# Order of small TensorE products in a two-layer hybrid decoder trunk on one core

## Chip, cores, metric

One NeuronCore of a Trainium2 chip runs the whole program. The metric is device time in microseconds (us) of one execution. All inputs and outputs are float32.

## What is computed

Two layers over 256 tokens and a width of 1024. The first half of each layer is a mixer with four parallel branches, the second half a gated feed-forward block:

```
for each of 2 layers:
  z  = rmsnorm(h) @ w_in            # columns: RWKV-7 | attention | mLSTM | HGRN2 | 4 gates
  y_b = mixer_b(z_b)                # four causal mixers, heads of width 64
  h += (sum_b sigmoid(gate_b) * (y_b @ P_b)) @ w_out
  h += conv_ffn(rmsnorm(h))
```

The RWKV-7 mixer is a recurrence over a 64x64 state per head, done here in four chunks of 64 tokens:

```
sa = S a_t ;  S = S * w_t + sa b_t + v_t k_t ;  y_t = S r_t
```

## The kernel before

**Main stream.** All large products go through `mm3` (lines 343 to 345). Each factor is split into a high and a low part, and three products are added: high times high, high times low, low times high. A weight group is loaded by SyncE's DMA queue, split by ScalarE (`hi`, L298) and VectorE (`lo`, L299) into one of four buffers each, up to three groups ahead of its use. These products (gate, at, ml, up, dn and so on) use the whole 128x128 array.

**Side work.** The mixers are Python generators: `rwkv`, `hgrn`, `attn`, `ml_gate` with `mlstm`. `step()` is called inside the main stream and advances them by a pace for each, up to the next `yield`. A list scheduler then sets the final order on each engine, and each engine runs its own list strictly from front to back. So a small product stands at a fixed place between main products, and TensorE waits there if its inputs are late.

**Shapes of the small products.** Two heads share a 128-partition tile: one has partitions 0 to 63, the other 64 to 127. A product whose contraction has 64 rows uses one half of the array's rows; one with 64 output partitions uses one half of its columns. A float32 product appears as two matmul records in the trace, a transpose and a main product as one.

**The places the change touches.** In `rwkv`: `pl` (L763), four blocks per layer, pair n of heads and head par, each four products of 64 rows by 128 columns, then the masked copy `LR` (L765) by VectorE. Then the chain over chunks j = 0 to 3 (L842 to L887): `prr` = a times state S (L848, 64 rows), the sum in `LV` (L849), `pu` (L858), its two copies into `UV`, `psS` (L867, 128 rows by 64 columns), the new S (L880, VectorE), and the output `pyy`. `pyy` adds r times S (L873, 64 rows) and LR times UV (L874, 128 rows) in one accumulation for each of four heads, and ScalarE copies it to `yt` (L886). PSUM for this branch is two banks (`RWB = 2`), for the other branches three.

In `hgrn`: `pdg` (L1023) and `pdl` for h = 64 and 128 (L1050, L1053), head after head; `qsb` (L999, L1002) by VectorE is an input of `pdl`. In `attn`: the scores `psA`, `psB` (L1136), head after head, with up to 256 keys in one product. In `mlstm`: the scores `pS` (L1261, L1262). `y_out` (L569 to L574) transposes the finished mixer outputs (`pyC`, `pyA`) and splits them into `yhC`, `ylC`, which the projection `pp` of the main stream reads.

Of the kernel before, what the change touches and what calls it, by code (L numbers as in the profile page):

```python
# [9 lines left out]
F32 = mybir.dt.float32  # L10
# [3 lines left out]
OP = mybir.AluOpType  # L14
# [205 lines left out]
def trunk(tc, x, wst, prm, rows, lora, fing, cfd, cid, out, dbg=None, depth=DEPTH):  # L220
# [9 lines left out]
    PS = {}  # L230
# [248 lines left out]
    for l in range(depth):  # L479
        with ExitStack() as lx:  # L480
# [11 lines left out]
            with ExitStack() as mxs:  # L492
# [129 lines left out]
                def rwkv():  # L622
# [133 lines left out]
                    LR = rw.tile([128, 2, 2, 4, 2, 64], F32, name="LR", tag="w8")  # L756
                    lm = C("lmask")[:, None, :].to_broadcast([128, 4, 128])
                    for n in range(2):
                        for par in range(2):
                            q0 = par * 64  # L760
                            pl = PS["rw"].tile([128, 4, 128], F32, name="pl", tag="rw")
                            for j in range(4):
                                te.matmul(pl[:, j, :], bk[q0:q0 + 64, n, j].rearrange("p a b -> p (a b)"),  # L763
                                          ar[q0:q0 + 64, n, j].rearrange("p a b -> p (a b)"), start=True, stop=True)
                            ve.tensor_tensor(LR[:, n, par].rearrange("p j a t -> p j (a t)"), pl, lm, op=OP.mult)  # L765
                            yield
# [74 lines left out]
                    S, py = None, None  # L841
                    for j in range(4):  # L842
                        Rs = LV[:, :, j, :]
                        if j:
                            prr = PS["rw"].tile([128, 2, 64], F32, name="prr", tag="rw")
                            for n in range(2):
                                for q in (0, 64):
                                    te.matmul(prr[q:q + 64, n, :], ar[q:q + 64, n, j, 0, :], S[q:q + 64, n, :], start=True, stop=True)  # L848
                            ve.tensor_tensor(Rs, Rs, prr, op=OP.add)  # L849
# [12 lines left out]
                        if j < 3:  # L862
                            psS = PS["rw"].tile([128, 2, 64], F32, name="psS", tag="rw")
# [4 lines left out]
                        py = PS["rw"].tile([128, 2, 64], F32, name="pyy", tag="rw")  # L868
# [65 lines left out]
                def hgrn(zz, sp):  # L934
# [80 lines left out]

                    pds = []
                    for par in range(2):
                        pd = PS["mx"].tile([128, 4, 64], F32, name="pdg", tag="mx")
                        pds.append(pd)
                        for e in range(4):  # L1020
                            for pj in range(2):
                                sl = slice(e * 128 + pj * 64, e * 128 + pj * 64 + 64)
                                te.matmul(pd[pj * 64:pj * 64 + 64, e, :], kfl[par * 64:par * 64 + 64, sl], qfl[par * 64:par * 64 + 64, sl],  # L1023
                                          start=True, stop=True)
                    for par in range(2):
                        for pj in range(2):
# [5 lines left out]
                    while h <= 128:  # L1032
# [9 lines left out]
                                              qs[:, e * 2 + pj].rearrange("p a t -> p (a t)"), start=True, stop=True)  # L1042
                        else:
                            for par in range(2):
                                r0 = par * 64
                                pd = PS["mx"].tile([128, 4, 128], F32, name="pdl", tag="mx")
                                pds.append(pd)
                                for e in range(4):
# [74 lines left out]
                def attn(zz, sp):  # L1123
                    qk, V = zz["qk"], zz["v"]
                    am = C("amask").rearrange("p (g s) -> p g s", g=3)

                    PTs = [sp.tile([128, 3, 384], F32, name=f"PT{j}") for j in range(2)]
                    for th, j in [(th, j) for th in range(2) for j in range(2)]:
                        n_ = 128 * (th + 1)
                        r0 = j * 64  # L1130
                        S = sp.tile([128, 3, 256], F32, name="S_at", tag="S_at", bufs=2)
                        psA = PS["mx"].tile([128, 512], F32, name="psA", tag="mx")
                        psB = PS["mx"].tile([128, 512], F32, name="psB", tag="mx") if th else None
                        for g in range(3):
                            dst = psA[:, g * n_:(g + 1) * n_] if (th == 0 or g < 2) else psB[:, 0:256]
                            te.matmul(dst, qk[r0:r0 + 64, g, th * 128:(th + 1) * 128], qk[r0:r0 + 64, 3 + g, 0:n_], start=True, stop=True)  # L1136
                        Sv = S[:, :, 0:n_]
                        if th == 0:
                            ve.tensor_tensor(Sv, psA[:, 0:384].rearrange("p (g s) -> p g s", g=3), am[:, :, 128:256], op=OP.add)
                        else:  # L1140
                            ve.tensor_tensor(Sv[:, 0:2, :], psA.rearrange("p (g s) -> p g s", g=2), am[:, 0:2, :], op=OP.add)
                            ve.tensor_tensor(Sv[:, 2, :], psB[:, 0:256], am[:, 2, :], op=OP.add)
# [97 lines left out]
                def mlstm(zz, sp):  # L1240
# [17 lines left out]
                    for hd in range(4):  # L1258
                        n, r0 = hd // 2, (hd % 2) * 64
                        pS = PS["mx"].tile([128, 512], F32, name="pS", tag="mx")  # L1260
                        te.matmul(pS[:, 0:256], cv[r0:r0 + 64, 2 + n, 0:128], cv[r0:r0 + 64, n, :], start=True, stop=True)  # L1261
                        te.matmul(pS[:, 256:384], cv[r0:r0 + 64, 2 + n, 128:256], cv[r0:r0 + 64, n, 128:256], start=True, stop=True)  # L1262
                        ve.scalar_tensor_tensor(W[:, hd, :], pS[:, 0:384], 0.125 * 0.25, W[:, hd, :], op0=OP.mult, op1=OP.mult)
                        if hd % 2:
                            yield
# [238 lines left out]
```

## Time and profile before

| | |
|---|---|
| median of 3 runs | 972.03 us (969.34 to 972.32) |
| the profiled execution | 971.28 us, of it 969.5 us span |
| TensorE busy | 948.9 us, 98% |
| VectorE busy | 738.7 us, 76% |
| ScalarE busy | 564.5 us, 58% |
| GpSimd busy | 231.5 us, 24% |
| granted TensorE clock, mean | 0.989 |

A matmul's recorded duration covers its way through the array, and records overlap. So the cost of a product is the distance from its start to the next start, and that is how all rows of TensorE are read below. The span minus the time of the run is 1.8 us outside the first and last instruction.

### The profile page before, as it was taken

To read this page: it belongs to the slowest core of one execution; us is meant where nothing else is said; L and a number is where in the kernel's file an instruction comes from. 1 tells how busy PE (TensorE), PEld (TensorE's weight loads), DVE (VectorE), ACT (ScalarE), POOL (GpSimd) and SP (SyncE) were. 2 spreads that over 40 slices of the span, in tenths; PEclk is the share of its full clock that TensorE was granted. 3 is DMA by queue.
4 is the path that set the end of the run, shared out by engine and by line. 5 is a ranking of instruction groups with operands and counts; after the bars stand their busy time and mean duration, and the time that the engine had idled before them with its cause. 6 is when DMAs were issued, how large, how long until landed. Compare 5 with 4: busy or idle time off the path is not lost.

```text
span 969.5 us, 21763 instructions
## 1 busy us (share of the span) xinstructions
PE 948.9 (98%) x8860; PEld 889.9 (92%) x8860; DVE 738.7 (76%) x1180; ACT 564.5 (58%) x953; POOL 231.5 (24%) x228
## 2 busy tenths in 40 slices
PE   7999999999999999999999999999999999999996
PEld 5989998989999999999998999898999999999885
DVE  6899765568688998876698986655787889888643
ACT  6874445555466676665578534455645667766533
POOL 3500221112207721110060004100222473111101
PEclk9999999999999999999999999999999999999999
DMA  7644353433456465556555344433345647655551
GB/s 256 198 145 149 106 164 120 142 117 129 158 186 212 146 221 196 196 185 201 192 189 169 126 133 149 132 132 121 113 147 186 204 136 225 197 191 192 190 190 65
DMA packets 48979, 160.08 MB, mean 165 GB/s; under 512 B 5872, under 2 KB 7408, under 8 KB 48752
## 3 DMA queue, kind: packets, MB, share of 16 engines
q1 hardware_dynamic: 46944, 155.55, 48.8%
q10 hardware_dynamic: 1584, 2.10, 0.7%
q8 instruction: 69, 1.13, 0.5%
q0 software_dynamic: 352, 1.06, 0.4%
q14 instruction: 30, 0.25, 0.1%
HBM read 156.06 MB, written 1.05 MB: 162 GB/s over the span
## 4 chain that ended last, share of the span: by engine, by line
PE 78%; DVE 9%; POOL 6%; ACT 2%; issue 2%; DMA 2%; SPq 0%; POOLq 0%; ACTq 0%; DVEq 0%
PE up L344 7%; PE up L345 7%; PE up L343 7%; PE gate L343 5%; PE gate L345 5%; PE gate L344 5%; PE dn L345 4%; PE dn L343 4%; PE dn L344 4%; POOL sl L438 4%; DVE lo L299 2%; POOL xsc L1381 2%; PE pp L343 1%; PE pp L345 1%; PE wo L344 1%
## 5 line engine op out<-in xcount | busy, mean ns | idle before, releaser
L299 DVE TENSOR_TENSOR lo<-raw,hi 128x1024 fp32r<-128x1024 f32 (+4 forms) x314 | 373.6, 1193 | 145.9 <-ACT hi L298 144.9
L298 ACT CAST hi<-raw 128x1024 fp32r<-128x1024 f32 (+4 forms) x314 | 308.3, 984 | 283.6 <-PE gate L344 69.1
L344 PE MATMUL up<-sl,hi 128*128 128x256 f32 x576 | 160.4, 279 | 3.6 <-POOL sl L438 3.5
L345 PE MATMUL up<-sh,lo 128*128 128x256 f32 x576 | 159.9, 278 | 0.0
L343 PE MATMUL up<-sh,hi 128*128 128x256 f32 x576 | 159.7, 278 | 0.0
L343 PE MATMUL gate<-sh,hi 128*128 128x256 f32 x512 | 147.3, 288 | 0.0
L345 PE MATMUL gate<-sh,lo 128*128 128x256 f32 x512 | 144.4, 282 | 0.0
L344 PE MATMUL gate<-sl,hi 128*128 128x256 f32 x512 | 144.1, 281 | 0.0
L344 PEld LDWEIGHTS up<-sl,hi 128*128 128x128 f32 x576 | 108.9, 189 | 4.6 <-POOL sl L438 4.6
L345 PEld LDWEIGHTS up<-sh,lo 128*128 128x128 f32 x576 | 108.9, 189 | 0.1
L343 PEld LDWEIGHTS up<-sh,hi 128*128 128x128 f32 x576 | 108.8, 189 | 0.0
L343 PEld LDWEIGHTS gate<-sh,hi 128*128 128x128 f32 x512 | 97.8, 191 | 3.2 <-issue 0.7
L345 PEld LDWEIGHTS gate<-sh,lo 128*128 128x128 f32 x512 | 97.7, 191 | 1.5 <-issue 0.8
L344 PEld LDWEIGHTS gate<-sl,hi 128*128 128x128 f32 x512 | 97.7, 191 | 0.5
L1406 POOL TENSOR_TENSOR af<-sf,cvf 128x256 f32<-128x256 f32 x44 | 42.6, 970 | 161.6 <-ACT sf L1404 161.5
L1402 DVE SCALAR_TENSOR_TENSOR cvf<-up,pr,cvf 128x255 f32<-128x255 f32 (+1 forms) x144 | 69.0, 479 | 2.6
L553 POOL TENSOR_TENSOR merged<-merged,gt 128x512 f32<-128x512 f32 x16 | 24.6, 1545 | 102.1 <-DVE gt L551 82.1
L345 PE MATMUL dn<-ahi,lo 128*128 128x256 f32 x176 | 48.5, 276 | 0.0
L344 PE MATMUL dn<-alo,hi 128*128 128x256 f32 x176 | 48.5, 276 | 0.0
L343 PE MATMUL dn<-ahi,hi 128*128 128x256 f32 x176 | 48.4, 276 | 0.0
L1399 ACT ACTIVATE cvf<-up,pr 128x256 f32<-128x256 f32 x72 | 40.4, 561 | 1.6 <-DVE cvf L1402 1.6
L438 POOL TENSOR_TENSOR sl<-xsc,sh 128x256 fp32r<-128x256 f32 x32 | 39.2, 1259 | 0.0
(466 smaller groups left out, 2377.0 us busy)
## 6 DMA issues: line engine op xcount, KB each, us to landing
raw<-in_wst_dram SPq DMA_DIRECT2D x254, 512.0 KB, 3.3
raw<-in_wst_dram SPq DMA_DIRECT2D x28, 256.0 KB, 2.9
raw<-in_wst_dram SPq DMA_DIRECT2D x16, 448.0 KB, 3.2
raw<-in_wst_dram SPq DMA_DIRECT2D x8, 392.0 KB, 3.1
zrot<-zrot ACTq DMA_DIRECT2D x24, 64.0 KB, 3.1
cft<-in_cf_dram SPq DMA_DIRECT2D x1, 1041.0 KB, 6.8
hT<-in_x_dram SPq DMA_DIRECT2D x4, 256.0 KB, 5.3
raw<-in_wst_dram SPq DMA_DIRECT2D x8, 128.0 KB, 2.4
```

Source lines behind the costliest of these rows:

```text
L298: ac.copy(hi[:, c], r[:, c])
L299: ve.tensor_tensor(lo[:, c], r[:, c], hi[:, c].bitcast(F32), op=OP.subtract)
L343: te.matmul(o, lh, rh, start=first, stop=False)
L344: te.matmul(o, lh, rl, start=False, stop=False)
L345: te.matmul(o, ll, rh, start=False, stop=last)
L438: gp.tensor_tensor(lo[:, m, :], tmp, h[:, m, :].bitcast(F32), op=OP.subtract)
L553: gp.tensor_tensor(mo, mo, g, op=OP.add)
L1381: gp.tensor_tensor(xsc[:, m, :], xsc[:, m, :], R, op=OP.mult)
L1399: ac.activation(cv[:, n, :], z[:, n, :], AF.Identity, bias=P("fcb", cj), scale=P("fcw", 88 + cj))
L1402: ve.scalar_tensor_tensor(cv[:, n, d:], z[:, n, 0:T - d], P("fcw", 44 * i + cj), cv[:, n, d:], op0=OP.mult, op1=OP.add)
L1406: gp.tensor_tensor(a_, s, cv[:, 0, :], op=OP.mult)
```

## The change

In the RWKV chain, `prr` and `pyy` share one bank (`pry`), and `pu` and `psS` another. Both products with the state (a times S and r times S) are issued in one run of eight; LR times UV follows later, after `psS`, and completes the second half. Elsewhere the products with 64 rows are issued so that the two heads alternate, each head into its own bank: `pl`, `pdg`, `pdl` for h at least 64, the attention scores (also cut to 128 keys each, with one more `yield`), and the mLSTM scores. No operation of VectorE, ScalarE or GpSimd is added.

```diff
                     for n in range(2):
+                        pls = [PS["rw"].tile([128, 4, 128], F32, name="pl", tag="rw") for _ in range(2)]
+                        for j in range(4):
+                            for par in range(2):
+                                q0 = par * 64
+                                te.matmul(pls[par][:, j, :], bk[q0:q0 + 64, n, j].rearrange("p a b -> p (a b)"),
...
                         for par in range(2):
-                            q0 = par * 64
-                            pl = PS["rw"].tile([128, 4, 128], F32, name="pl", tag="rw")
-                            for j in range(4):
...
+                            ve.tensor_tensor(LR[:, n, par].rearrange("p j a t -> p j (a t)"), pls[par], lm, op=OP.mult)
+                        yield
+                        yield
...
+                        pry = PS["rw"].tile([128, 2, 2, 64], F32, name="prr", tag="rw")
+                        py = pry[:, 1]
                         if j:
-                            prr = PS["rw"].tile([128, 2, 64], F32, name="prr", tag="rw")
...
+                            for a in range(2):
+                                for n in range(2):
+                                    for q in (0, 64):
+                                        te.matmul(pry[q:q + 64, a, n, :], ar[q:q + 64, n, j, a, :], S[q:q + 64, n, :],
+                                                  start=(a == 0 or n == 0), stop=(a == 0))
+                            ve.tensor_tensor(Rs, Rs, pry[:, 0], op=OP.add)
...
-                        pu = PS["rw"].tile([128, 2, 64], F32, name="pu", tag="rw")
+                        pus = PS["rw"].tile([128, 2, 2, 64], F32, name="pu", tag="rw")
+                        pu, psS = pus[:, 0], pus[:, 1]
...
                         for n in range(2):
                             for par in range(2):
                                 q = par * 64
-                                if j:
-                                    te.matmul(py[q:q + 64, n, :], ar[q:q + 64, n, j, 1, :], S[q:q + 64, n, :], start=True, stop=False)
-                                te.matmul(py[q:q + 64, n, :], LR[:, n, par, j, 1, :], UV[:, j, n, par, :], start=(j == 0), stop=True)
+                                te.matmul(py[q:q + 64, n, :], LR[:, n, par, j, 1, :], UV[:, j, n, par, :], start=(j == 0), stop=(j == 0 or n == 1))
...
+                    for e in range(4):
+                        for pj in range(2):
+                            sl = slice(e * 128 + pj * 64, e * 128 + pj * 64 + 64)
+                            for par in range(2):
+                                te.matmul(pds[par][pj * 64:pj * 64 + 64, e, :], kfl[par * 64:par * 64 + 64, sl], qfl[par * 64:par * 64 + 64, sl],
...
+                    def scores(th, sb, Ss):
+                        pa = [PS["mx"].tile([128, 3, 128], F32, name="psA", tag="mx") for _ in range(2)]
+                        for g in range(3):
+                            for j in range(2):
+                                r = slice(j * 64, j * 64 + 64)
+                                te.matmul(pa[j][:, g, :], qk[r, g, th * 128:(th + 1) * 128], qk[r, 3 + g, sb * 128:(sb + 1) * 128],
...
+                    for n in range(2):
+                        pSs = [PS["mx"].tile([128, 512], F32, name="pS", tag="mx") for _ in range(2)]
+                        for c in range(2):
+                            for par in range(2):
+                                te.matmul(pSs[par][:, c * 256:256 + c * 128], cv[r, 2 + n, c * 128:c * 128 + 128], cv[r, n, c * 128:], start=True, stop=True)
```

Line numbers shift: `psS` is L875 in the changed kernel and bears the name of its bank, `pu`; r times S and a times S are L855, LR times UV is L879, both named `prr`.

**TensorE, RWKV chain, chunk 1 of layer 0.** The rows are instructions in program order, with the line, the operation, the tile written and the tiles read, and a count of products. `ml` and `mlt` are main products. Before:

```order
L345 MATMUL ml_2547<-sh,lo_2480 128x256
L867 MATMUL psS<-UV,bkT 64x64 x4
L873 MATMUL pyy<-S,ar 64x64
L874 MATMUL pyy<-UV,LR 64x64
L873 MATMUL pyy<-S,ar 64x64
L874 MATMUL pyy<-UV,LR 64x64
```

and two more such pairs. Now:

```order
L345 MATMUL ml_2556<-sh,lo_2485 128x256
L875 MATMUL pu<-UV,bkT 64x64 x4
L879 MATMUL prr<-UV,LR 64x64 x4
L343 MATMUL mlt_2638<-hi_2514,sh 128x512
L344 MATMUL mlt_2638<-lo_2515,sh 128x512
```

The products with S have moved ahead of `pu`, into one run of eight (`L855 ... x8`), and the eight products after `UV` stand in one run without a change of form.

**VectorE, end of the HGRN2 levels, layer 0.** `qsb_900` is the input of the last `pdl` (h = 128), `lo` a weight split, `qkat` the attention's rotated q and k. Before:

```order
L789 COPY_PREDICATED TT<-cit,LR 32x256 x2
L1002 TENSOR_TENSOR qsb_900<-zhq,thf 128x256
L792 STREAM_TRANSPOSE T__1430<-TT 128x256
L299 TENSOR_TENSOR lo_1451<-raw_1343,hi_1450 128x1024
L1112 TENSOR_TENSOR qkat<-at_1342,cft 128x512
```

Now:

```order
L998 TENSOR_TENSOR kt_839<-zhf,Q 128x2x128
L299 TENSOR_TENSOR lo_1451<-raw_1349,hi_1450 128x1024
L1118 TENSOR_TENSOR qkat<-at_1348,cft 128x512
L1007 TENSOR_TENSOR qsb_900<-zhq,thf 128x256
L299 TENSOR_TENSOR lo_1481<-raw_1379,hi_1480 128x784
```

The last `qsb` has moved behind a weight split and behind `qkat`; the copies `TT` and the transpose stand earlier.

**TensorE, end of the mLSTM and RWKV branches, layer 0.** Before:

```order
L343 MATMUL gate_3263<-sh,hi_3193 128x256
L569 MATMUL pyC<-ident_t,y_ml 128x128
L569 MATMUL pyA<-ident_t,yt 128x128 x2
L569 MATMUL pyC<-ident_t,y_ml 128x128 x3
L569 MATMUL pyA<-ident_t,yt 128x128 x2
L344 MATMUL gate_3263<-sl,hi_3193 128x256
```

Now:

```order
L345 MATMUL gate_3263<-sh,lo_3194 128x256
L569 MATMUL pyC<-ident_t,y_ml 128x128
L569 MATMUL pyA<-ident_t,yt 128x128 x4
L569 MATMUL pyC<-ident_t,y_ml 128x128 x3
L343 MATMUL pp_3334<-yhC,hi_3223 128x256
L343 MATMUL pp_3355<-yhC,hi_3266 128x256
L343 MATMUL gate_3370<-sh,hi_3296 128x256
```

The transposes have moved 23 main products later, to the place directly ahead of the first product that reads `yhC`.

## Rows read from the trace of the kernel before

**Rows 1.** Page: busy us (share of the span) and number of instructions, by engine.

```profile
PE 948.9 (98%) x8860; PEld 889.9 (92%) x8860; DVE 738.7 (76%) x1180; ACT 564.5 (58%) x953; POOL 231.5 (24%) x228
```

**Rows 2.** Windows: stretch, length, then busy us (count) of PE, PEld, DVE, ACT, POOL.

```profile
48.00:108.00 60.00, 59.58 (x542) 53.52 (x540) 57.93 (x119) 33.65 (x60) 1.04 (x2) 1.00 0.43 139
173.00:224.00 51.00, 51.00 (x410) 44.13 (x409) 31.26 (x59) 28.18 (x51) 8.19 (x8) 0.98 0.38 125
```

**Rows 3.** Waits of TensorE from 30 to 960 us: total us, times, longest.

```profile
PE pdl L1040 <- DVE qsb L999: 0.9, 3, 0.4
```

**Rows 4.** Timeline of TensorE around `prr`: start us, duration, instruction, forms, records.

```profile
181.85 0.28 PE L344 MATMUL ml<-sl,hi 128*128 128x256 f32 x1
181.97 0.28 PE L345 MATMUL ml<-sh,lo 128*128 128x256 f32 x1
182.17 0.45 PE L848 MATMUL prr<-S,ar 64*64 64x64 f32 x8
182.55 0.38 PE L343 MATMUL ml<-sh,hi 128*128 128x256 f32 x1
182.77 0.29 PE L344 MATMUL ml<-sl,hi 128*128 128x256 f32 x1
```

**Rows 5.** Timeline of TensorE, state and output of chunk 1, layer 0.

```profile
190.16 0.45 PE L867 MATMUL psS<-UV,bkT 128*64 128x64 f32 x8
190.54 0.32 PE L873 MATMUL pyy<-S,ar 64*64 64x64 f32 x2
190.80 0.33 PE L874 MATMUL pyy<-UV,LR 128*64 128x64 f32 x2
...
192.60 0.51 PE L343 MATMUL mlt<-hi,sh 128*128 128x512 f32 x1
```

**Rows 6.** Timeline of TensorE, HGRN2 after the last level, layer 0.

```profile
105.93 0.72 PE L1053 MATMUL pdl<-qsb,kt 64*128 64x128 f32 x8
106.58 0.69 PE L1079 MATMUL po<-Vh,A 128*64 128x64 f32 x16
107.19 1.05 PE L776 MATMUL psq<-cft,prod 128*128 128x2 f32 x8
```

**Rows 7.** Timeline of ScalarE during chunk 1, layer 0.

```profile
191.22 0.59 ACT L1181 COPY z<-ml 128x512 f32<-128x512 f32 x1
192.70 0.53 ACT L886 COPY yt<-pyy 64x128 f32<-64x128 f32 x2 [0.89 <-PE pyy L874]
```

**Rows 8.** Timeline of TensorE, one `pl` block of the first layer.

```profile
85.04 1.16 PE L763 MATMUL pl<-ar,bk 64*128 64x128 f32 x8
86.12 0.38 PE L343 MATMUL gate<-sh,hi 128*128 128x256 f32 x1
```

**Rows 9.** Timeline of TensorE, `pdg` of the first layer.

```profile
65.60 0.98 PE L1023 MATMUL pdg<-zhq,zhf 64*64 64x64 f32 x32
66.51 0.39 PE L343 MATMUL gate<-sh,hi 128*128 128x256 f32 x1
```

**Rows 10.** Timeline of VectorE at the end of the HGRN2 levels.

```profile
105.45 0.43 DVE L1002 TENSOR_TENSOR qsb<-zhq,thf 128x256 f32<-128x256 f32 x1
...
107.25 0.68 DVE L1112 TENSOR_TENSOR qkat<-at,cft 128x512 f32<-128x512 f32 x1
```

**Rows 11.** Timeline of TensorE, attention scores of one head, first and second query block.

```profile
133.57 0.93 PE L1136 MATMUL psA<-qkat 64*128 64x128 f32 x6
134.44 0.75 PE L805 MATMUL pd<-X,TT 32*32 32x32 f32 x64
...
146.89 1.13 PE L1136 MATMUL psA<-qkat 64*128 64x256 f32 x4
147.86 0.59 PE L1136 MATMUL psB<-qkat 64*128 64x256 f32 x2
148.38 0.38 PE L343 MATMUL gate<-sh,hi 128*128 128x256 f32 x1
```

**Rows 12.** Timeline of ScalarE, the split of the mLSTM output.

```profile
248.40 0.59 ACT L573 ACTIVATE yhC<-pyC 128x512 fp32r<-128x512 f32 x1
```

More of the change, by code (lines that the diff above doesn't have):

```diff
@@ L758, in rwkv @@
                     for n in range(2):
-                        for par in range(2):
-                            q0 = par * 64
-                            pl = PS["rw"].tile([128, 4, 128], F32, name="pl", tag="rw")
-                            for j in range(4):
[L763 to L766, printed above, removed]
+                        pls = [PS["rw"].tile([128, 4, 128], F32, name="pl", tag="rw") for _ in range(2)]
[3 more added lines that the diff above has]
+                                te.matmul(pls[par][:, j, :], bk[q0:q0 + 64, n, j].rearrange("p a b -> p (a b)"),
+                                          ar[q0:q0 + 64, n, j].rearrange("p a b -> p (a b)"), start=True, stop=True)
+                        for par in range(2):
+                            ve.tensor_tensor(LR[:, n, par].rearrange("p j a t -> p j (a t)"), pls[par], lm, op=OP.mult)
+                        yield
+                        yield
                     bkT = rw.tile([128, 2, 4, 128], F32, name="bkT", tag="w4a")
@@ L840, in rwkv @@
                     yt = rw.tile([128, 2, 4, 64], F32, name="yt", tag="w2a")
-                    S, py = None, None
+                    S = None
                     for j in range(4):
                         Rs = LV[:, :, j, :]
+                        pry = PS["rw"].tile([128, 2, 2, 64], F32, name="prr", tag="rw")
+                        py = pry[:, 1]
                         if j:
-                            prr = PS["rw"].tile([128, 2, 64], F32, name="prr", tag="rw")
[L846 to L849, printed above, removed]
+                            for a in range(2):
[4 more added lines that the diff above has]
+                            ve.tensor_tensor(Rs, Rs, pry[:, 0], op=OP.add)
                         if j:
@@ L862, in rwkv @@
                         if j < 3:
-                            psS = PS["rw"].tile([128, 2, 64], F32, name="psS", tag="rw")
                             for n in range(2):
@@ L867, in rwkv @@
                                     te.matmul(psS[q:q + 64, n, :], bkT[:, n, j, q:q + 64], UV[:, j, n, par, :], start=True, stop=True)
-                        py = PS["rw"].tile([128, 2, 64], F32, name="pyy", tag="rw")
                         for n in range(2):
@@ L1017, in hgrn @@
                     for par in range(2):
[L1018 to L1023, printed above, removed]
+                        pds.append(PS["mx"].tile([128, 4, 64], F32, name="pdg", tag="mx"))
+                    for e in range(4):
[3 more added lines that the diff above has]
+                                te.matmul(pds[par][pj * 64:pj * 64 + 64, e, :], kfl[par * 64:par * 64 + 64, sl], qfl[par * 64:par * 64 + 64, sl],
                                           start=True, stop=True)
@@ L1044, in hgrn @@
                             for par in range(2):
[L1045 to L1048, printed above, removed]
+                                pds.append(PS["mx"].tile([128, 4, 128], F32, name="pdl", tag="mx"))
+                            for e in range(4):
+                                for par in range(2):
+                                    r0 = par * 64
+                                    pd = pds[par]
                                     if h == 64:
@@ L1127, in attn @@
                     PTs = [sp.tile([128, 3, 384], F32, name=f"PT{j}") for j in range(2)]
+                    def scores(th, sb, Ss):
[4 more added lines that the diff above has]
+                                te.matmul(pa[j][:, g, :], qk[r, g, th * 128:(th + 1) * 128], qk[r, 3 + g, sb * 128:(sb + 1) * 128],
+                                          start=True, stop=True)
+                        m0 = 128 + (sb - th) * 128
+                        for j in range(2):
+                            ve.tensor_tensor(Ss[j][:, :, sb * 128:(sb + 1) * 128], pa[j], am[:, :, m0:m0 + 128], op=OP.add)
@@ L1128, in attn @@
                     for th, j in [(th, j) for th in range(2) for j in range(2)]:
                         n_ = 128 * (th + 1)
[L1130 to L1136, printed above, removed]
@@ L1137, in attn @@
-                        Sv = S[:, :, 0:n_]
[L1138 to L1142, printed above, removed]
+                        if j == 0:
+                            Ss = [sp.tile([128, 3, 256], F32, name="S_at", tag="S_at", bufs=2) for _ in range(2)]
+                            for sb in range(th + 1):
+                                if sb:
+                                    yield
+                                scores(th, sb, Ss)
@@ L1143, in attn @@
+                        S = Ss[j]
+                        Sv = S[:, :, 0:n_]
                         mx = sp.tile([128, 4], F32, name="mx_at", tag="mx_at", bufs=2)
@@ L1257, in mlstm @@
                     W, cols = go["W"], go["cols"]
[L1258 to L1265, printed above, removed]
+                    for n in range(2):
+                        pSs = [PS["mx"].tile([128, 512], F32, name="pS", tag="mx") for _ in range(2)]
+                        for c in range(2):
+                            for par in range(2):
+                                r = slice(par * 64, par * 64 + 64)
+                                te.matmul(pSs[par][:, c * 256:256 + c * 128], cv[r, 2 + n, c * 128:c * 128 + 128], cv[r, n, c * 128:], start=True, stop=True)
+                        for par in range(2):
+                            hd = n * 2 + par
+                            ve.scalar_tensor_tensor(W[:, hd, :], pSs[par][:, 0:384], 0.125 * 0.25, W[:, hd, :], op0=OP.mult, op1=OP.mult)
+                        yield
                     y = sp.tile([128, 2, 256], F32, name="y_ml", tag="th_ml")
```

## The prediction

> **What bounds the kernel now.** Read the page's first line, then the windows, then TensorE's waits. The page has TensorE busy for 98% of the span, ScalarE for 58% [rows 1]. A busy TensorE proves little, since records overlap; what proves it is that nothing is waited for: from 30 to 960 us the side products that sit between main products wait for VectorE at `pdl` alone, 0.9 us in all [rows 3]. So in most of the span time is the sum of the distances from one start to the next on TensorE, and a microsecond that leaves its list leaves the run. One stretch is different. From 48 to 108 us VectorE is busy for 57.93 of 60 us, against 31.26 of 51 us later [rows 2]. There two engines are full at once, and a gain of TensorE can go no further than VectorE follows.
>
> Next the price of a side trip. A main product starts 0.12 us after the one ahead of it (181.85 to 181.97). A run of eight `prr` records starts 0.20 us after the last main product, lasts 0.38 us to the next main start, and that main product takes 0.22 us instead of 0.12 [rows 4]. So entering and leaving another form costs some 0.19 us beside the run.
>
> **The chain (4.65 us a layer).** Chunk 1: `psS` takes 0.38 us for eight records. Then come eight pieces of two records, S products and LR products in turn, from 190.54 to 192.60 us, 0.257 us each [rows 5]. Eight records without a change of form cost 0.38 us, so four fifths of the two microseconds are the changes between 64 and 128 rows. In the changed order `psS` and LR times UV have one form, 128 rows by 64 columns, 16 records in a row. A run of just that shape and length exists: `po`, 0.61 us (106.58 to 107.19) [rows 6]. So 2.44 us (190.16 to 192.60) become 0.61. The r times S products join the run of eight before; 16 records for 8 cost 0.61 less 0.38, 0.23 us more. Net 1.60 us for chunk 1 and the same for chunk 2. Chunk 3 has no `psS`: 2.06 becomes 0.38, less 0.23, net 1.45. Chunk 0 has no state: nothing. Sum 4.65 us a layer.
>
> What is late next? The next `prr` now shares its bank with the output, so it waits for ScalarE's `yt` copies, and less time separates them: 20 main products, some 2.3 us, from the output to the next run with S. In the trace the copy of z ends at 191.8 and the two `yt` copies take 0.53 us together [rows 7]; without the wait for the old output they end near 192.3, 2.2 us after `psS` starts at 190.16, while the new run with S is due 0.61 and 2.3 us after it, at 2.9 us. Cover of 0.7 us: I cost this at nothing. If a weight cast of about 1 us slips ahead, the cover is gone by 0.3 us, behind which the main stream would stand.
>
> **`pl` and the HGRN2 products (1.3 us a layer).** Eight records of one head take 1.08 us [rows 8]. The trace already holds two heads with this very shape: `pdl` for h = 128, four records for each head, takes 0.65 us [rows 6]. By the difference a further record of one head costs 0.108 us, so four of one head alone would take 0.65 us too: the second head is free. Hence 16 records in turn cost 1.08 us. Layer 0 has four trips of 1.27 us before and two after, minus 2.54 us; in layer 1 the first pair is cut in two by main products, which leaves 2.13. For `pdg` 32 records take 0.91 us [rows 9], an estimate of 0.65 us with both heads in turn, and a like 0.25 us for h = 64. Together TensorE loses about 3.0 us a layer, but all of it inside the stretch in which VectorE has 2.07 us of idle time in 60 [rows 2]. Moreover the last `qsb`, which ended at 105.9 us, now stands behind a weight split and behind `qkat`, which ended at 107.9 [rows 10]; the last `pdl`, its reader, started at 105.93 [rows 6]. In the new order that `pdl` has two runs of `po` and other work behind it instead of ahead, so the delay is partly paid out of the saving. Bounds: 0, if VectorE yields nothing, and 3.0, if its order loosens fully. I take 1.3, nearer the idle time of VectorE than the whole.
>
> Here a rule speaks: the Trainium skill, "TensorE: Matmul & The Clock Gate", Part 3 (packing small matmuls), says that matmuls start and end strictly in program order, and only weight loads are pulled ahead. `pdl` for h = 128 is written head after head before; by that rule its eight records would cost as much as `pl`'s, 1.08 us, and alternation would bring 0.43 us a layer there. The rows show 0.65, so the trace does not agree and the sum has nothing for it.
>
> **Attention scores (1.1 us a layer).** One head's first block is six records, 0.87 us (133.57 to 134.44); its second, six records of twice the length, 1.49 us (146.89 to 148.38) [rows 11]. Both heads: 4.72 us. Now there are three blocks of 12 records, each 0.87 us by the pairing above, if in one run. The new order cuts two of them, by `pd` or by main products: 0.65 and 0.43, 0.65 and 0.65, and one whole, 3.25 us. The order also has two more trips (a score block in two, the product `poa` in one more piece), 0.38 us. Net 4.72 less 3.63, 1.1 us; bounds 0.5 and 1.7. Mask additions and softmax are the same operations on VectorE, which has room here.
>
> **mLSTM scores (0).** The second pair of heads does not get two banks at once from three; in the new order its two heads stand apart by main products, as before. The first pair stands close enough in the old order to overlap as `pdl` did. Bounds minus 0.2 and plus 0.5 us.
>
> **A new wait (minus 0.8 us a layer).** `pyC` now stands directly ahead of the projection that reads `yhC`. ScalarE's copy takes 0.59 us [rows 12] and can start only when the last transpose is through the array, some 0.2 us. Until now 23 main products covered this. What is queued behind the waiting product is the whole main stream. I take 0.8; bounds 0 and 1.8, the latter if one weight cast of ScalarE stands ahead.
>
> **Sum.** 4.65 + 1.3 + 1.1 + 0 - 0.8 = 6.25 us a layer, 12.5 us for two. The second half of each layer is unchanged and in step with TensorE, so the shift carries to the end. The profiled execution took 971.3 us (span 969.5 and 1.8 around it), which gives 958.8; against the median of 972.0 it is 959.5. I say 959.
>
> **Rivals.**
>
> The stretch of `pl` yields all: VectorE idles less and TensorE's full 3.0 us count, and scores and the wait at `yhC` fall on their good sides. 4.65 + 3.0 + 1.7 + 0.5 = 9.85 us a layer, 952 us. For it: weight splits are early there. Against it: 57.93 of 60.
>
> The pairing does not hold, or the chain's cover does not: heads that alternate through one half of the rows each gain nothing where both write all columns, or `prr` waits for `yt`. Then the chain alone counts, 4.65 less up to 0.3 for each of three chunks, less 0.8 to 1.8 for `yhC`: 2 to 3.9 us a layer, 964 to 968 us. Against it: `pdl` at 0.65 us.
>
> Nothing changes: the run is bound elsewhere, 970 to 974 us. For this the 98% would have to be waiting in disguise; the uniform 0.12 us speaks against it.
>
> Slower: VectorE between 48 and 108 us (520 and 578 in layer 1). It works its list in order, and each microsecond in which it stands at a `pl` or `pdl` that TensorE has not reached is a microsecond of the run, as it has no reserve. The paired `LR` copies wait for 16 records instead of 8, and the order of the levels has moved. The price is one for one; it decides once VectorE stands still for more than 6.25 us a layer beyond today's 2.07. Ten places of 1 us each would give 980 us. Today's waits there are far from that.
>
> **How the numbers follow.** Chances: the forecast (955 to 963) 0.62, the full yield (950 to 955) 0.12, the half yield (963 to 969) 0.16, nothing (within 0.3%, 2.9 us, about what a measurement of this kernel can tell) 0.06, slower 0.04. The range that leaves out no more than 2 in 10 goes from 951 to 966: below it is the sum of the upper bounds, 952, and one for the scatter of runs; above it is the sum of the lower bounds, (4.65 - 0.9 + 0 + 0.5 - 0.2 - 1.8) x 2 = 4.5 us or 967, cut by one. Faster by over 0.3% has the first three, 0.90.
>
> **What would show it.** Right: L879 and L875 in one run of 0.6 us with no pieces of 0.26; `pl` with 16 records in about 1.1 us; TensorE waiting about 1 us for `yhC` L573; VectorE still over 95% busy until the last `pdl`. Wrong: a wait of L855 for `yt` of more than 0.3 us, `pl` at 2.1 us for 16 records, or waits of TensorE for `qsb` that add up to more than 2 us a layer.

## The result, and the profile after

The changed kernel takes 963.00 us, median of 11 runs (957.52 to 971.25), beside 972.32 us for the kernel before (968.42 to 976.75). The ratio is 0.9917, 95% interval 0.9891 to 0.9944. A second set gave 961.69 beside 971.57 us, ratio 0.9892 (0.9857 to 0.9927). So 9.3 to 9.9 us are gone. Forecast were 959 us and 12.5 us less: right in sign and inside the range from 951 to 966 us, at the upper edge of the forecast's own band (955 to 963), and too large by a quarter to a third.

The page's first line answers to [rows 1]; TensorE has 12 us less of busy time, the other engines are within 4 us of what they were.

```profile
PE 936.8 (97%) x8884; PEld 882.9 (91%) x8884; DVE 741.9 (77%) x1180; ACT 560.9 (58%) x953; POOL 231.8 (24%) x228
```

The profiled execution itself took 969.59 us, well above the median. Ahead of any comparison one has to see why. Two windows of 40 us in layer 0's feed-forward, where nothing was changed, before and after (columns as in [rows 2]):

```profile
380.00:420.00 40.00, 40.00 (x355) 40.00 (x354) 33.20 (x51) 26.73 (x45) 6.62 (x7) 1.00 0.59 196
```

```profile
380.00:420.00 40.00, 40.00 (x342) 40.00 (x341) 32.19 (x51) 25.49 (x42) 6.61 (x7) 1.00 0.56 184
```

355 main products before, 342 now, both at a granted clock of 1.00: the step from one start to the next is 0.1133 us before and 0.1178 us now. In this execution the longer step holds from about 305 to 505 us and costs 6.6 us. In a second profile of the same kernel (e1_again, below) it is not there. So stages are compared, not whole spans. A stage is the time from the first product of one main group to the first of the next, read from TensorE's timeline; a group bears the name of the tile that it writes, as `hgt` or `att`:

| stage (us) | layer | before | after | e1_again |
|---|---|---|---|---|
| hgt to att (`pl`, HGRN2) | 0 | 73.79 | 73.02 | 73.22 |
| | 1 | 73.41 | 72.96 | 73.44 |
| pp to ml (attention) | 0 | 44.98 | 43.79 | 43.73 |
| | 1 | 44.98 | 44.79 | 44.28 |
| ml to mlt (chunk 1) | 0 and 1 | 15.52 | 13.94 | 13.94 |
| mlt to wo (chunks 2, 3, `pS`, `yhC`) | 0 | 85.79 | 83.24 | 83.23 |
| | 1 | 85.78 | 83.00 | 83.01 |
| up to layer 1's rw (unchanged) | 0 | 183.66 | 190.26 | 185.87 |

The four changed stages of both layers sum to 11.1 us less after, 11.0 in e1_again. What lies outside the table took 346.1 us before, 348.0 after and 348.9 in e1_again; it scatters between executions, from 343.1 to 348.9 us over the profiles of e1 to e5 and e8 to e10, whichever kernel ran.

**The chain.** Chunk 1 of layer 0, answering to [rows 5]:

```profile
189.24 0.45 PE L875 MATMUL pu<-UV,bkT 128*64 128x64 f32 x8
189.52 0.40 PE L879 MATMUL prr<-UV,LR 128*64 128x64 f32 x8
189.85 0.51 PE L343 MATMUL mlt<-hi,sh 128*128 128x512 f32 x1
```

From 189.24 to 189.85 us: 0.61 instead of 2.44, as forecast.

**Pairing.** `pl`, answering to [rows 8], `pdg` to [rows 9], the last `pdl` to [rows 6]:

```profile
79.92 1.16 PE L764 MATMUL pl<-ar,bk 64*128 64x128 f32 x16
81.01 0.39 PE L343 MATMUL gate<-sh,hi 128*128 128x256 f32 x1
```

```profile
66.38 0.69 PE L1028 MATMUL pdg<-zhq,zhf 64*64 64x64 f32 x32
67.00 0.38 PE L343 MATMUL gate<-sh,hi 128*128 128x256 f32 x1
...
108.62 0.72 PE L1059 MATMUL pdl<-qsb,kt 64*128 64x128 f32 x8
109.27 0.69 PE L1085 MATMUL po<-Vh,A 128*64 128x64 f32 x16
```

16 records of two heads take 1.09 us, the time that 8 of one head took: the second head is free. `pdg`, with 16 records of each head, fell from 0.91 to 0.62. The last `pdl`, with only four of each, takes 0.65 in turn as it took head after head, so there the halves had overlapped already. By the rule of the Trainium skill that the prediction weighed ("TensorE: Matmul & The Clock Gate", Part 3, strict program order) 0.43 us should have come out here, and nothing did: the trace does not agree with it.

**The waits.** Total, times, longest, answering to [rows 3]; then the stretch in which VectorE is full, answering to the first of [rows 2]:

```profile
PE pdl L1045 <- DVE qsb L1004: 3.0, 3, 1.9
PE pp L343 <- ACT yhC L573: 2.7, 2, 1.4
...
PE pdl L1056 <- DVE qsb L1007: 0.7, 2, 0.4
...
PE pdl L1059 <- DVE qsb L1007: 0.2, 1, 0.2
```

```profile
48.00:108.00 60.00, 57.82 (x531) 52.66 (x530) 57.79 (x119) 34.16 (x61) 1.32 (x2) 0.97 0.44 139
```

TensorE is 1.8 us less busy there than before, VectorE is as full: part of what the pairing freed is now waited for at `qsb`, 3.9 us in both layers beside 0.9 before.

The place at `yhC`, answering to [rows 12]; ScalarE's list, with TensorE's last transposes and its waiting product:

```profile
243.03 1.05 ACT L298 CAST hi<-raw 128x1024 fp32r<-128x1024 f32 x1 [1.67 <-PE gate L344]
...
243.49 0.49 PE L569 MATMUL pyC<-ident_t,y_ml 128*128 128x128 f32 x3
243.98 0.83 ACT L531 ACTIVATE gt<-gate,hpar 128x256 f32<-128x256 f32 x2
...
244.71 0.60 ACT L573 ACTIVATE yhC<-pyC 128x512 fp32r<-128x512 f32 x1
...
245.36 0.51 PE L343 MATMUL pp<-yhC,hi 128*128 128x256 f32 x2 [1.37 <-ACT yhC L573]
```

A weight cast and two gate activations stand ahead of the copy; TensorE stands for 1.37 us. By their records the transposes end at 243.98 us and the cast at 244.08, only 0.1 us later; from then until 244.71 the copy stands behind the two activations.

**The clock.** Windows of 4 us, layer 0: before, and after at the same place and at 87 us.

```profile
222.00:226.00 4.00, 4.00 (x23) 4.00 (x23) 3.67 (x9) 2.76 (x5) 0.00 (x0) 0.57 0.23 87
```

```profile
222.00:226.00 4.00, 4.00 (x38) 4.00 (x37) 4.00 (x7) 4.00 (x5) 3.05 (x1) 1.00 0.51 155
...
87.00:91.00 4.00, 4.00 (x28) 3.88 (x25) 3.97 (x7) 0.00 (x0) 0.00 (x0) 0.58 0.36 133
```

Before, the clock was at 1.2 GHz for 3.4 us behind the broken-up output of chunk 3, in both layers; after, this is gone, and it falls behind the wait of 1.9 us at `pdl` in layer 0 instead. The prediction had neither. Neither is shown to be the cause: other executions below have the same order without the fall.

### The profile page after: what moved, and what is told of

The parts are those of the page before. It is cut to its first block, busy times and chain, and to the rows that moved or that the text cites. A ratio compares the mean times of both kernels' runs of the same rounds, so it can differ in the third digit from the quotient of the medians.

```text
span 967.0 us, 21817 instructions
## 1 busy us (share of the span) xinstructions
PE 936.8 (97%) x8884; PEld 882.9 (91%) x8884; DVE 741.9 (77%) x1180; ACT 560.9 (58%) x953; POOL 231.8 (24%) x228
## 3 DMA queue, kind: packets, MB, share of 16 engines
HBM read 156.06 MB, written 1.05 MB: 162 GB/s over the span
## 5 line engine op out<-in xcount | busy, mean ns | idle before, releaser
L299 DVE TENSOR_TENSOR lo<-raw,hi 128x1024 fp32r<-128x1024 f32 (+4 forms) x314 | 379.2, 1212 | 150.7 <-ACT hi L298 149.5
L553 POOL TENSOR_TENSOR merged<-merged,gt 128x512 f32<-128x512 f32 x16 | 34.4, 2152 | 88.8 <-DVE gt L551 86.2
```

Of the source, the lines that this page charges most:

```text
L299: ve.tensor_tensor(lo[:, c], r[:, c], hi[:, c].bitcast(F32), op=OP.subtract)
L553: gp.tensor_tensor(mo, mo, g, op=OP.add)
```

## Experiments

**e1_again.** No edit.

> The changed kernel once more, unaltered, for a second profile. In its first profile the step from one main product to the next was 0.1178 us instead of 0.1133 from about 300 to 500 us (layer 0's feed-forward), where nothing was changed; that alone is some 7.5 us of its 967.0 us span. Theory (this stretch belongs to the execution, not to the kernel): it lies elsewhere or is absent now, and the mixer of each layer, from the first at product to the first wo product, again takes 4.5 to 5.5 us less than before (156.75 us before in both layers). Rival (the change brings it about): the slow steps stand again between 300 and 500 us, and the time stays near 969. Median of the timed runs: 962 to 965 by the theory.

Measured: 961.69 us; the long step is absent from 320 to 475 us (355 products from 380 to 420 us); the stages repeat to within 0.5 us. The long stretch belongs to the execution, as the theory said.

**The three parts alone.** e2_chain, e3_attn and e4_plhg are the kernel before with only that hunk of the diff.

> The kernel before with the RWKV chain's part of the change alone. Its order of instructions has the transposes of y_ml directly ahead of the first product that reads yhC, as the whole change has. Theory (the chain carries nearly all, and the wait at yhC comes with it): ml to mlt 13.94 us in both layers (15.52 before), mlt to wo 83.0 us (85.8 before), the wait for yhC 1.35 us a layer is there, and the granted clock, which before falls to 0.5 for 3.3 us near 222 and 693 us, stays at 1.00 there: 4.2 us a layer, 963 to 965 us. Rival (the clock is kept up by the alternating heads, not by the chain): the clock falls near 222 us again and 1.4 us a layer is missing, 966 to 967 us. Second rival (the whole forecast of 4.65 us a layer less 0.8 arrives, and the rest of the gain is elsewhere): mlt to wo is 2.25 us shorter.

> The kernel before with the attention scores' part alone: two heads in turn, blocks of 128 keys. Theory (the profile of the whole change): from the first pp to the first ml product 44.98 us becomes 43.8 in layer 0 and 44.8 in layer 1, since waits in layer 1 take back what TensorE saves: 1.4 us in all, 970.5 us. Rival (the forecast): 1.1 us in each layer, 2.2 us in all, 969.8 us. Second rival (pairing does nothing for blocks with 128 columns): two more side trips and no gain, 0.4 us a layer more, 973 us. The stage's length in the profile decides, since the medians scatter by more than the difference.

> The kernel before with pl, pdg and pdl alternating the heads, and nothing else. Theory (VectorE is the bound in this stretch): TensorE's 3.0 us a layer come out as 0.4 to 0.8 us from the first hgt product to the first att product, and TensorE waits for qsb 1.5 us a layer or more instead of 0.45, in layer 0 long enough that the granted clock falls to 0.5 for some 3 us near 87 us: 970.5 to 971.5 us in all. Rival (the forecast): 1.3 us a layer, 969.4 us. Second rival (full yield): 3.0 us a layer, 966 us.

| stage less before (us) | e2_chain | e3_attn | e4_plhg |
|---|---|---|---|
| hgt to att, layer 0, 1 | 0.0, 0.0 | 0.0, +0.2 | -0.8, -0.2 |
| pp to ml | 0.0, 0.0 | -1.0, -1.0 | 0.0, 0.0 |
| ml to mlt | -1.58, -1.58 | 0, 0 | 0, 0 |
| mlt to wo | -2.55, -2.52 | -1.35, +0.2 | -1.60, 0.0 |
| median, ratio | 968.86, 0.9955 (0.9928 to 0.9981) | 971.01, 0.9983 (0.9956 to 1.0011) | 970.09, 0.9978 (0.9951 to 1.0006) |

The chain's part alone brings the wait at `yhC`: 2.7 us, as in the whole change. Its stages came as expected, its median did not: its twelve runs lie in two groups, 962.7 to 966.1 and 968.5 to 971.1, and the profiled one (970.78) holds the long step, from about 330 to 500 us. Attention alone gives 1.0 us in each layer, so there the rival holds and the theory fell: the 0.2 and 0.7 us of layer 1 in the whole change belong to executions. In the first the trips with `px` and `pt` are 0.5 and 0.4 us longer than elsewhere, in e1_again one with `psA` and `pd` is 0.3 us longer. e4 bears out its theory, apart from layer 1's gain of 0.2 us: 0.8 us in layer 0, 4.1 us of waits for `qsb` in both layers, and the clock falls at 85.5 us. In the row mlt to wo, e3 and e4 have the old chain and yet 1.35 and 1.60 us less in layer 0: there the clock did not fall near 222 us. So its fall costs 1.35 to 1.6 us. Over all profiles it fell near there in 5 of 10 layers with the old chain, in 3 of 12 with the changed one, in none of 6 with e8's. That the chain's part prevents it is not shown; some 3 of the 11.0 us of the stages are its fall in the one profile of before.

**e8_grouped.** The kernel before with the output's products regrouped, at the old place:

```diff
+                        for n in range(2) if j else ():
+                            for par in range(2):
+                                q = par * 64
+                                te.matmul(py[q:q + 64, n, :], ar[q:q + 64, n, j, 1, :], S[q:q + 64, n, :], start=(n == 0), stop=False)
                         for n in range(2):
                             for par in range(2):
                                 q = par * 64
-                                if j:
-                                    te.matmul(py[q:q + 64, n, :], ar[q:q + 64, n, j, 1, :], S[q:q + 64, n, :], start=True, stop=False)
-                                te.matmul(py[q:q + 64, n, :], LR[:, n, par, j, 1, :], UV[:, j, n, par, :], start=(j == 0), stop=True)
+                                te.matmul(py[q:q + 64, n, :], LR[:, n, par, j, 1, :], UV[:, j, n, par, :], start=(j == 0), stop=(j == 0 or n == 1))
```

> The kernel before with one thing changed in the chain: the four products r times S of a chunk are issued in a row and then the four LR times UV, instead of in turn; place, banks and all else stay. Theory (the price is that of changing between 64 and 128 rows): seven of the eight changes go, eight records cost 0.38 us each way and one change 0.1 to 0.2 more, so the output of chunk 1 takes 0.9 us instead of 2.06 and ml to mlt 14.3 to 14.5 us instead of 15.52. Rival (the price is that of finishing an accumulation, each pair of products waiting for the other in the same piece of the bank): ml to mlt stays at 15.3 to 15.5.

```profile
189.62 0.45 PE L867 MATMUL psS<-UV,bkT 128*64 128x64 f32 x8
190.00 0.45 PE L872 MATMUL pyy<-S,ar 64*64 64x64 f32 x8
190.38 0.45 PE L876 MATMUL pyy<-UV,LR 128*64 128x64 f32 x8
190.76 0.51 PE L343 MATMUL mlt<-hi,sh 128*128 128x512 f32 x1
```

The output takes 0.76 us instead of 2.06, ml to mlt 14.23; the one run took 966.82 us, and its profile holds the long step. The price is that of alternating in pieces of two records. The sum alone does not refute the rival, since in the new order four products lie between the two that add up in one piece of the bank. Single records of the kernel before do: where LR times UV adds to what S has just written, its first record starts 0.149 us after the one ahead; where the form changes and nothing is added up, from `psS` to the first S and from LR to the next S, it is 0.152 us. So accumulation costs nothing on top of the change of form. The order in turn had a second cost: every piece held one product alone, while in a run of four two products with different output halves start 0.007 us apart. Grouping ends both, and what each of them is worth was not measured apart.

Side trips of layer 0, in which TensorE leaves the main products for small ones (each from the start of the last main product ahead to the next main start), show where each kernel gains:

| trips (us) | before | after | e8_grouped |
|---|---|---|---|
| chunk 1: `prr`, behind UV | 0.58, 2.64 | 0.82, 0.82 | 0.58, 1.35 |
| chunk 2, with `pg` | 0.70, 3.08 | 0.94, 0.47, 0.87 | 0.70, 1.78 |
| chunk 3, with `pu`, `pm`, `pc` | 0.58, 0.98, 0.64, 3.42 | 0.82, 0.58, 0.36, 1.54, 1.09 | 0.58, 0.98, 0.64, 2.52 |
| mLSTM scores | 1.71, 1.05 | 1.71, 1.05 | 1.71, 1.05 |
| `pyC`, `pyA` up to `pp` | 0.91 | 2.52 | 0.91 |

The changed chain saves 1.58 + 1.50 + 1.23 = 4.31 us and loses 1.61 at `yhC`; the grouping saves 1.29 + 1.30 + 0.90 = 3.49 and loses nothing, since its order leaves the transposes 23 main products ahead.

**e5_early_yhc.** The changed kernel, mLSTM steps taken with a priority 60 instructions earlier:

```diff
-                    next(e[0])
+                    if len(e) > 3:
+                        with tc.high_priority(offset=e[3]):
+                            next(e[0])
+                    else:
+                        next(e[0])
...
-                bg.append([gm, PACE[2], 0])
+                bg.append([gm, PACE[2], 0, 60])
```

> The changed kernel, with the mLSTM branch put 60 instructions earlier in the scheduler's order, so that the transposes of y_ml stand 45 to 57 main products ahead of the first product that reads yhC instead of directly ahead of it. Theory (the wait at yhC is what the new order costs): the 1.37 us a layer of TensorE at yhC are gone, and mlt to wo takes 81.7 to 82.0 us instead of 83.0 to 83.2; 2.5 us less in all than the changed kernel's 962.5, 960. Rival (the wait only moves on): the next late value, yhA or the gates of the last group, takes its place, mlt to wo stays above 82.8. A small loss in both: one run of eight products with S is cut by two main-form products, 0.3 us a layer.

Measured: 966.95 us, ratio 0.9938 (0.9904 to 0.9973). No wait for `yhC` is left, but mlt to wo takes 85.53 and 84.96 us: 24 side trips of 17.77 us instead of 14 of 14.87, for the new order scatters `pu`, `pg` and the chain's runs between main products. The wait went, and more than it cost came back as trips: theory and rival both fell.

**e6_relief, e7_relief_before.** Changed kernel and kernel before, with four weight groups of each layer subtracted by GpSimd:

```diff
-ve.tensor_tensor(lo[:, c], r[:, c], hi[:, c]..., op=OP.subtract)
+(gp if i % 157 in (15, 18, 21, 24) else ve).tensor_tensor(lo[:, c], ...)
```

> The changed kernel, with the low part of four of the weight groups of each layer that are split between 48 and 108 us subtracted by GpSimd instead of VectorE. That takes 4 x 1.2 us of VectorE's work out of the stretch in which it is full. Theory (VectorE is what held back the gain of pl and the HGRN2 products): from the first hgt to the first att product 71.0 to 71.7 us instead of 73.0, TensorE waits less than 1 us for qsb, and the granted clock does not fall near 87 us: 3 to 4 us less in all than the changed kernel, 959. Rival (TensorE's own list sets this stretch, VectorE only looks full): 72.7 to 73.2 as now. Second rival (GpSimd takes so long over 1024 columns, 5 us by four times the 1.26 us of sl, that main products wait for lo): above 73.5.

> The kernel before with the same four weight groups subtracted by GpSimd. Theory (VectorE is the bound there): with the reserve, TensorE's list alone sets the stretch in both kernels, so what e6_relief is shorter by from hgt to att is now what TensorE saves, 1.5 to 2.5 us a layer, instead of the 0.2 to 0.7 us that the part gave without the reserve; the stage takes 73.0 to 73.8 us here. Rival (the saving of TensorE itself is as small as what arrived): the difference stays at 0.2 to 0.7 us.

e6 took 985.34 us, ratio 1.0101 (1.0021 to 1.0181), and its hgt to att 80.82 and 82.45 us; e7 81.96 and 81.03 (one run, 990.53). Both theories fell. The length is that of e6's second rival (above 73.5), but not by its way: no main product waits for `lo`; TensorE waits 15.9 us at `pdl` for VectorE's `A` and `qsb`. VectorE, then GpSimd, in e6:

```profile
63.37 2.88 DVE L713 TENSOR_TENSOR zr<-zr,km 128x512 f32<-128x512 f32 x1
...
75.67 2.90 DVE L1004 TENSOR_TENSOR qsb<-zhq,thf 64x256 f32<-64x256 f32 x2
```

```profile
62.90 2.80 POOL L299 TENSOR_TENSOR lo<-raw,hi 128x1024 fp32r<-128x1024 f32 x1 [8.95 <-ACT hi L298]
75.76 2.54 POOL L299 TENSOR_TENSOR lo<-raw,hi 128x1024 fp32r<-128x1024 f32 x1 [10.06 <-ACT hi L298]
```

The same product `zr` takes 0.68 us in the changed kernel; here it ends only after GpSimd's subtraction has. What GpSimd takes over, VectorE loses standing. VectorE has thus lost time here instead of gaining it, so the experiment does not test what a reserve of VectorE would bring.

**e11_act_after, e12_act_before.** The same four low parts as a plain ScalarE copy:

```diff
-            ve.tensor_tensor(lo[:, c], r[:, c], hi[:, c].bitcast(F32), op=OP.subtract)
+            if i % 157 in (15, 18, 21, 24):
+                ac.copy(lo[:, c], r[:, c])
+            else:
+                ve.tensor_tensor(lo[:, c], r[:, c], hi[:, c].bitcast(F32), op=OP.subtract)
```

> The changed kernel, with the low part of four weight groups of each layer (those of e6_relief) written by ScalarE as a plain copy of the weight, not as the remainder after rounding; the output is therefore not the reference's, and the time is that of a kernel whose VectorE has 4 x 1.2 us a layer less to do in the stretch where it is full, without GpSimd's long subtractions. Theory (VectorE is the bound there): hgt to att 70.5 to 72.0 us, 1.5 to 2.5 us less than e12_act_before in each layer, and TensorE waits less than 1.5 us in all for qsb. Rival (TensorE has no more to save there than what arrived): 0.2 to 0.7 us less than e12_act_before.

> The kernel before with the same four low parts a layer written by ScalarE as a copy of the weight (the output is not the reference's). Theory (VectorE is the bound in the changed kernel, TensorE's list is not far behind it in the kernel before): hgt to att 73.0 to 73.5 us, hardly less than the 73.4 to 73.8 of before, since TensorE's list is as long as it was. Rival (VectorE alone sets the stretch in both kernels): both get shorter by the same 1 to 3 us.

One run each: e11 965.81 us, e12 975.05. hgt to att: e11 73.46 and 73.04, e12 74.27 and 74.53 us. The difference is 0.8 and 1.5 us, between theory and rival, and neither kernel got shorter: with lighter VectorE the scheduler moves the levels of HGRN2 ahead on TensorE, and TensorE waits 6.1 us for `qsb` in e11. Undecided by this pair.

**e9_grouped_attn, e10_grouped_all.** e8 with the attention part, and that with `pl`, `pdg`, `pdl` too.

> The kernel before with two things: in the chain only the grouping of e8_grouped (four r times S, then four LR times UV, at the old place), and the attention scores' part of the change. pl, the HGRN2 and the mLSTM products stay head after head. Theory (the stages add up): ml to mlt 14.23, mlt to wo 82.2, pp to ml 44.0 in both layers, no wait at yhC; 1.29 + 3.54 + 1.0 = 5.8 us a layer less than before, 11.7 in all, 960 us, 2 to 3 us ahead of the changed kernel. Rival (much of the 3.54 us was the clock that did not fall in that one execution, 1.4 us a layer, and it falls again here): mlt to wo 83.6, 963 us.

> e9_grouped_attn with pl, pdg and pdl alternating the heads as well. Theory (VectorE holds that stretch back, and the wait for qsb in layer 0 is long enough to bring the clock down): hgt to att 73.0 and 73.2 us as in the changed kernel, 0.2 to 0.7 us a layer less than without, so 959 to 960 us, not told apart from e9_grouped_attn by the medians. Rival (the part pays by itself once the chain is shorter): 2 us or more less than e9_grouped_attn.

e9: 962.92 us, ratio 0.9897 (0.9860 to 0.9935); the stages are as expected (ml to mlt 14.23, mlt to wo 82.00 and 81.99, pp to ml 43.97 and 44.16), and the profiled execution again held the long step; the median stands 3 us above the 960 expected. e10: **959.44 us**, 955.20 to 960.73, ratio 0.9871 (0.9838 to 0.9905), the fastest kernel here; the intervals do not part it from e9 or from the changed kernel, the stages do: in ml to wo it takes 0.7 us a layer less than the changed kernel. e10 also bears on VectorE. Its instructions between 48 and 108 us stand in the changed kernel's order, with the same longest wait of 1.9 us at `pdl`, but the clock stayed at 1.00, against what was expected. The stretch, then the waits for `qsb`:

```profile
48.00:108.00 60.00, 56.62 (x549) 51.24 (x548) 57.63 (x120) 33.14 (x60) 2.23 (x3) 1.00 0.44 139
```

```profile
PE pdl L1045 <- DVE qsb L1004: 3.9, 4, 1.9
...
PE pdl L1056 <- DVE qsb L1007: 1.0, 2, 0.6
...
PE pdl L1059 <- DVE qsb L1007: 0.2, 1, 0.2
```

Layer 0's hgt to att takes 72.86 us, with the clock's fall 73.02, although the fall costs 1.35 us or more elsewhere: TensorE waits for `qsb` instead (5.1 us in all against 3.9). So in this order the arrival of VectorE's `qsb` ends that stage, and not TensorE's own list. Whether VectorE's load or only the order of its list sets that arrival stays open: in e11 VectorE is busy for 54.64 of the same 60 us, and the stage is no shorter.

## Why the prediction was right in part

**Chain, forecast 4.65, got 4.31 a layer.** Chunk 1 came to within 0.02 us. Chunks 2 and 3 gave 1.50 and 1.23 for 1.60 and 1.45: `pg` and `pc`, which had ridden along in the old runs, now make trips of their own. The working put the price to the changes between 64 and 128 rows alone; that in turn no two output halves run side by side is part of it, by e8's records. No wait of L855 for `yt` appears; the cover of 0.7 us held.

**`pl` and HGRN2, forecast 1.3, got about 0.55** (0.6 to 0.9 less in layer 0, 0.5 less to none in layer 1, over the profiles of after, e1, e4, e5 and e10). Two things failed. The step that took 1.3 between the bounds 0 and 3.0, as what VectorE's order would yield, was too generous: a `pdl` that the new order puts 16 main products earlier waits 1.9 us for `qsb`. And layer 1's first `pl` pair was counted as alternating in two halves; the order has four products of one head, three main products, four of the other, so nothing is paired there, and each half takes 1.09 us:

```profile
554.24 1.16 PE L764 MATMUL pl<-ar,bk 64*128 64x128 f32 x8
555.33 0.38 PE L343 MATMUL gate<-sh,hi 128*128 128x256 f32 x1
...
555.87 1.16 PE L764 MATMUL pl<-ar,bk 64*128 64x128 f32 x8
556.95 0.38 PE L343 MATMUL gate<-sh,hi 128*128 128x256 f32 x1
```

**Attention, forecast 1.1, got 1.0** alone; 0.2 to 1.25 within the change, 0.9 on average over after, e1 and e5. The size is partly luck. The working had the last block of scores as two halves with both heads in each, 0.65 us each; in the changed order its two heads stand apart, and each takes the unpaired 0.87 us:

```profile
145.75 0.93 PE L1140 MATMUL psA<-qkat 64*128 64x128 f32 x6
146.61 0.39 PE L343 MATMUL gate<-sh,hi 128*128 128x256 f32 x1
...
147.51 0.93 PE L1140 MATMUL psA<-qkat 64*128 64x128 f32 x6
148.38 0.38 PE L343 MATMUL gate<-sh,hi 128*128 128x256 f32 x1
```

With that the sum would have given 0.7. The term was also wrong in the number of trips, 17 in e3 against 12 before and not two more; where the other 0.3 us came from was not worked out.

**mLSTM scores, forecast 0, got 0**, to the hundredth.

**`yhC`, forecast minus 0.8, got minus 1.6.** The loss came near the term's upper bound of 1.8, but the weight cast that was to bring it ends only 0.1 us after the transposes. The copy itself takes 0.60 us, as counted; 0.6 to 0.7 us more went to the two gate activations, which the term did not have. I took ScalarE's list as empty without having read its order there.

Without the clock that is 4.31 + 0.55 + 0.9 - 1.6 = 4.2 us a layer, 8.4 in all, against 12.5; the clock's fall near 222 and 693 us, in half of the old chain's layers and a quarter of the changed one's, is worth some 0.7 us more on average. That makes 9.1, beside 9.3 and 9.9 measured, each known to about 3 us either way. Of what would show it: the single run, `pl` at 1.1 us, VectorE over 95% (57.79 of 60 us) and the wait at `yhC` (1.37 for about 1 us) were there. So was one sign of being wrong: waits for `qsb` stand at 1.95 us a layer, just under the stated limit of 2, and above it in e1_again of the same kernel (4.5 us in all) and in e10.

## What to carry over

Small TensorE products of different row counts cost by their changes of form: group them in runs, and let products on different row halves or output halves follow each other, before thinking of merging steps. Where a merge makes an order move, look at the first reader of every value that moves, and at what stands ahead of its producer on its own engine: here grouping alone gave up 0.8 us of trips a layer and kept 1.6. Where two engines are full at once, as here between 48 and 108 us, a saving on one can be found again as a wait for the other.

## What the runs showed of the hardware

- The step between main products has two levels at a granted clock of 1.00, 0.1133 and 0.1178 us, each held over many products. Six of fourteen profiles held the longer from between 305 and 330 to about 500 us, some 6 to 7 us a time, and shorter stretches of it stand in others; VectorE's, ScalarE's and GpSimd's instructions took as long as ever (the cast of 128x1024 1.05 us in both). What sets it stays open.
- A GpSimd subtraction of two 128x1024 operands takes 2.55 us on average, and a two-operand VectorE instruction that starts within it ends only after it (0.68 becomes 2.88 us). The Trainium skill, "SBUF — State Buffer", section "SBUF: two separate sides", has this as an exclusive lock on a port pair held for a whole instruction; the trace agrees.
- A fall of the granted clock to one half lasted 3.4 us and so lost 1.7 us of full-speed time; between 30 and 950 us every profile but e10's has at least one. In e6 and e7 some of these lasted twice as long. Main products then start 0.21 us apart.
